# Moving the forget gate and the first head's maxima among the attention projections

## The chip, the core and the metric

The kernel runs on one core of one Trainium2 chip. Its engines work side by side: TensorE (PE: matrix products, PEld: the loading of weights), VectorE (DVE), ScalarE (ACT), GpSimd (POOL) and SyncE (SP, which mostly issues transfers). The metric is the device time of one execution in microseconds (us), as a median over runs.

## The reference, cut to what matters

One layer of a hybrid encoder, with 1024 frames of width 1024. From one normalised input `h` come three groups, whose outputs go through an output projection and a mixture of experts:

```
h = rms_norm(x); proj = h @ w_in
ya = rglru_group(...)               # gated linear recurrence, width 256
yb = fox_group(q, k, v, fl, ...)    # attention with a forget gate, 8 heads of 64
yc = rwkv7_group(...)               # delta rule with a matrix state, 4 heads of 64
x  = x + concat(ya, yb, yc) @ w_out
x  = x + hier_moe(rms_norm(x))

# inside fox_group
qh, kh = rms_norm(q), rms_norm(k)                 # per head
log_f  = log_sigmoid(f_logit + fb)                # 8 logits per frame
c      = cumsum(log_f, axis=1)                    # over the frames
s      = qh @ kh.T * scale + c[query] - c[key]
p      = softmax(where(key <= query, s, -inf));  o = p @ v
```

The change touches only when the 8 logits, their running sums `c` and the row maxima of the first head's scores are computed.

## The kernel before, in words

The RWKV group is worked in two passes, `rwkv(0)` and `rwkv(1)` (line 400), of two heads each. A pass begins with elementwise work on DVE and ACT (from the decay's sigmoid L420 and its running sum, the scan L422, to the products L445 to L455), then takes 8 groups of products L467, whose results DVE masks (L470), turns blocks (L477), and inverts 32 small triangular matrices at once by 31 dependent pairs of DVE operations (L485, L487: "the inverse"). The inverse goes out to DRAM and comes back in another layout (L490, L509, L514), DVE turns it (L519), and PE combines its parts (L523, L528, L537). Then comes the recurrence over 16 chunks: L578, L580, L586, L587, L588, L591, L595, L597, L599, each waiting for the one before on another engine, and at the end the output (L567, L616, L617).

A pass leaves PE much idle time. So PE's stream is written out by hand: `dense()` (line 872) is a generator of other work for PE, the filler, and `dfill(t)` (line 902) takes from it, between two steps of the pass, as much as the step's yield names. A step of the recurrence yields 0.75 (`WC`), and takes 8 matmuls. What a piece overshoots is not carried over to the next step. PE runs in program order; the order on the other engines is made by a scheduler from priorities, in which the steps of the pass stand ahead of the filler.

The last part of the filler is six attention projections in the order q0, k0, v0, q1, k1, v1 (`attn_proj`, line 728; 0 and 1 are heads 0 to 3 and 4 to 7). Each has 8 tiles `t` of 128 frames, 24 matmuls L741 a tile, 192 in all. After each quarter come the norm or the copy of its results (L760 to L776, L751 to L754), through 4 PSUM banks (`PB`) that the projections share with the pieces below. `mids` are pieces that run just ahead of a tile `t`; `FMT` says at which tiles of each projection, and `seq` in which order they come:

- `lru_norm1`, `lru_norm2` (L703): the recurrence group's norm. `lru_norm2` transposes 2 x 4 tiles (L708) into two banks in turn, and DVE multiplies with them (L710).
- `forget1` (L781): the logits, 128 small matmuls L790, then on ACT and DVE the softplus (L795 to L797, and L258 to L278 inside `softplus`: 27 operations on DVE), which ends in the tile `spf`. It yields 4.0.
- `forget2` (L804): the running sums, L807 and L808 on `spf`; on DVE 7 dependent additions L812 and L814 to L818.
- `forget3` (L822): their transposes (L826), copied by L828 and stored to DRAM (`crd`, L829).
- `fload0` (L844): loads the first head's queries and keys, transposed (L847 to L851), from what the projections q0 and k0 and `forget3` stored.
- nine pieces `fmax0` (L854): scores of the first head (L861), reduced by DVE to row maxima (L864).
- `wo_first`: loads weights of the output projection.

After the last filler come the attention heads: `fox_pre` loads the first head's operands in SP's queue (L947 to L957, among them `q3` and `kh`, which lie in space that the RWKV passes had), `fox_shift` closes the maxima (L983), `fox_max` starts on the next head (L968), `fox_av` forms scores (L996, L997) and `fox_pv` multiplies with the values (L1025).

Of the kernel before, what the change touches and what calls it, by code (L numbers as in the profile page):

```python
# [39 lines left out]
W3 = 1.6  # L40
W2 = 1.0
FMC = (((7, 0),), ((7, 1),), ((6, 0),), ((6, 1), (0, 0)), ((5, 0),), ((5, 1), (1, 0)), ((4, 0),), ((4, 1), (2, 0)), ((3, 0),))
FMT = ((2,), (4,), (0, 5), (0, 2, 7), (1, 3, 5, 7), (0, 1, 3, 5, 6))
NPS = ()
FSM = False
WC = 0.75
# [66 lines left out]
def hybrid_layer(ctx: ExitStack, tc: tile.TileContext, d, out):  # L113
# [255 lines left out]
    def low_rank():  # L369
        ps = yield from inproj_T(0)  # L370
        lr = Q()
        shifted(ps, 0, lr)
        A.activation(lr[0:32], lr[0:32], AF.Tanh)
        A.activation(lr[64:128], lr[64:128], AF.Sigmoid)
        for j, (a, b, c) in enumerate(((0, 32, 64), (32, 64, 64), (64, 128, 0))):
            A.activation(ls[a:b, j], lr[a:b], AF.Copy, scale=LS)
            V.scalar_tensor_tensor(ls[c:c + b - a, j], lr[a:b], LS, ls[a:b, j], op0=ALU.mult, op1=ALU.subtract)
        V.tensor_copy(ls[32:64, 0], ls[0:32, 0])
        V.tensor_copy(ls[0:32, 1], ls[32:64, 1])

    def in_k(ct, res, mids={}):
        kt_ = T(pr, [P, S], F32, "kraw")
        ps = yield from inproj_T(1 + 3 * ct, mids)
        shifted(ps, 1 + 3 * ct, kt_)
        res[ct] = [kt_, None, None]

    def in_r(ct, res, mids={}):
        rt_ = T(pr, [P, S], F32, "rraw")
        ps = yield from inproj_T(2 + 3 * ct, mids)
        shifted(ps, 2 + 3 * ct, rt_)  # L390
        res[ct][1] = rt_

    def in_v(ct, res, mids={}):
        vt_ = T(pr, [P, CH + S], F32, "vt")
        G.memset(vt_[:, 0:CH], 0.0)
        ps = yield from inproj_T(3 + 3 * ct, mids)
        shifted(ps, 3 + 3 * ct, vt_[:, CH:])
        res[ct][2] = vt_
# [243 lines left out]
    def gate_a(ct):  # L642
        ps = PB2()
        mm2(ps, wab[:, ct], xcs[ct], 0, P)
        for hf in range(2):
            A.activation(rs_[ct][:, HS[hf]], ps[hf], AF.Sigmoid, bias=vec("ba", ct))
        yield 1.7
# [24 lines left out]
    def lru_out(ct):  # L672
        ps = yield from inproj_T(9 + ct)
        r = rs_[ct]
        for hf in range(2):
            A.activation(r[:, HS[hf]], ps[hf], AF.Gelu_apprx_tanh, scale=1.0 / WS)
        V.tensor_tensor(hss[ct], hss[ct], r, op=ALU.mult)
# [194 lines left out]
    def dense():  # L872
        yield from low_rank()
        yield from in_k(0, ins)
        yield from in_r(0, ins)
        yield from in_v(0, ins)
        yield from lru_x(0)
        yield from lru_x(1)
        ga = [{MK[0]: lambda c=c: gate_a(c), MK[1]: lambda c=c: gate_b(c)} for c in range(2)]
        yield from in_k(1, nxt, ga[0])  # L880
        yield from in_r(1, nxt, ga[1])
        yield from lru_out(0)
        yield from lru_out(1)
        yield from in_v(1, nxt)
        ins[1] = nxt[1]
        yield from lru_norm()
        fm = [lambda c=c: fmax0(*c) for c in FMC]
        seq = [lru_norm1, lru_norm2, forget1, forget2, forget3, fload0] + fm + [wo_first]
        i = 0
        for j, (a, b) in enumerate(((0, 0), (1, 0), (2, 0), (0, 1), (1, 1), (2, 1))):  # L890
            m = {}
            for t in FMT[j]:
                m[t] = seq[i]
                i += 1
            yield from attn_proj(a, b, m)
        fst["post"] = seq[i:]
        wload_o(3)
# [941 lines left out]
```

## Time and profile before

| | |
|---|---|
| median of 3 runs | 911.71 us (910.83 to 913.49) |
| the profiled execution | 909.1 us, of which its span 907.3 us |
| busy in the span: PE, DVE | 823.9 us (91%), 631.0 us (70%) |
| busy in the span: ACT, POOL | 502.3 us (55%), 291.9 us (32%) |
| mean granted clock of PE | 0.945 of full speed |
| the pass `rwkv(1)` in the span, with the six projections as filler | from about 230 to 416 us |

A profile gives each engine's busy time; "idle before <- releaser" beside a row is the time for which an engine stood still before it, and what ended that. PEclk is the clock that was granted to PE: 1.00 is 2.4 GHz, 0.50 is 1.2 GHz. The page's chain of what ended last has here only the last transfer, so it says nothing of the stretch in question; the tables by window and the timelines do.

### The profile page before, as it was taken

Reading aid. Unit: us, or ns where it says so; the run is one execution under the profiler, and the core shown is the slowest. Engines: PE = TensorE matmul, PEld = TensorE weight load, DVE = VectorE, ACT = ScalarE, POOL = GpSimd, SP = SyncE. Lnnn points to the kernel's source line nnn. Section 1 sums busy time; section 2 is a strip of 40 time slices with the busy share of each in tenths; the row PEclk is TensorE's granted clock in tenths of the full one; section 3 lists DMA queues with packets and bytes.
Section 4 is the critical chain, followed back from the end, with each engine's and each line's share of the span. In section 5 each row is a group of like instructions: output and inputs, shape, how many; then the busy total and the mean of one; then the engine's idle time right before and its main releaser. Section 6 shows DMA issues by size and latency. Waiting matters only on the chain. (4 is left out here: it accounts for less than half of the span.)

```text
span 907.3 us, 19706 instructions
## 1 busy us (share of the span) xinstructions
PE 823.9 (91%) x8028; PEld 566.2 (62%) x8028; DVE 631.0 (70%) x1366; ACT 502.3 (55%) x776; POOL 291.9 (32%) x222
## 2 busy tenths in 40 slices
PE   7999989999979699999799999889699999999992
PEld 5644445447757577767466556545478788788771
DVE  6858973534699914555578987588949888868640
ACT  6772456554743133433677778676536766767730
POOL 1000001165372431430334443400034455566351
PEclk9999997999999789999899999989779999999996
DMA  9201030111021260215967755888736999999862
GB/s 332 66 25 47 24 72 11 47 48 48 24 84 38 78 119 25 71 48 123 239 150 162 165 130 122 310 314 327 297 108 239 340 351 357 339 357 346 262 97 46
DMA packets 98130, 144.95 MB, mean 160 GB/s; under 512 B 52544, under 2 KB 73920, under 8 KB 91888
## 3 DMA queue, kind: packets, MB, share of 16 engines
q1 hardware_dynamic: 89520, 117.71, 40.8%
q0 software_dynamic: 8080, 25.17, 11.5%
q8 instruction: 65, 1.06, 0.5%
q10 hardware_dynamic: 432, 0.74, 0.2%
q14 instruction: 33, 0.27, 0.1%
HBM read 97.54 MB, written 35.18 MB: 146 GB/s over the span
## 5 line engine op out<-in xcount | busy, mean ns | idle before, releaser
L741 PE MATMUL pb<-w,h 128*128 128x256 f16 x1152 | 147.7, 281 | 0.0
L1535 PE MATMUL pg<-tg,e 128*128 128x192 f16 x1536 | 137.5, 248 | 0.0
L1535 PEld LDWEIGHTS <-e 128*128 128x128 f16 x1536 | 126.9, 99 | 6.2 <-issue 5.8
L333 PE MATMUL pb<-h,w 128*128 128x512 f16 x528 | 129.7, 390 | 0.0
L741 PEld LDWEIGHTS <-h 128*128 128x128 f16 x1152 | 110.6, 101 | 22.2 <-issue 2.2
L1187 DVE SCALAR_TENSOR_TENSOR e<-est,go,e 128x2048 f16<-128x2048 f32 x36 | 83.5, 2346 | 2.5 <-ACT e L1186 2.5
L333 PEld LDWEIGHTS <-w 128*128 128x128 f16 x528 | 49.0, 100 | 56.4 <-issue 8.1
L1186 ACT ACTIVATE e<-est,go 128x2048 f16<-128x2048 f32 x36 | 70.8, 1995 | 17.7 <-PE pg L1535 17.2
L1011 POOL TENSOR_TENSOR ptl<-pfx,pth 128x512 f16<-128x512 f32 (+1 forms) x48 | 49.6, 1033 | 78.7 <-ACT pth L1010 45.8
L1001 ACT ACTIVATE pfx<-s,bia 128x512 f32<-128x512 f32 (+1 forms) x96 | 55.9, 582 | 32.1 <-PE s L997 19.3
L1472 POOL DMA_INDIRECT g<-td,gi x16 | 24.9, 1558 | 113.3 <-DVE oh L1315 73.3
L1590 POOL DMA_INDIRECT out_dram<-ya,si x16 | 39.5, 2471 | 61.7 <-ACT ya L1589 58.9
L1065 PE MATMUL op<-w,y 128*128 128x512 f16 x192 | 59.3, 391 | 0.0
L971 DVE TENSOR_REDUCE mx<-m 128x1 f32<-128x512 f32 (+2 forms) x84 | 44.7, 552 | 16.1 <-PE m L970 12.4
L245 POOL TENSOR_SCALAR wst<-wst 128x1024 f32<-128x1024 f32 x12 | 34.7, 2896 | 57.1 <-DMA wst<-in_wq_dram 56.8
L1484 ACT COPY tg<-tr 128x1024 f16<-128x1024 f16 (+2 forms) x34 | 26.5, 800 | 43.7 <-PE tr L1490 43.6
L1595 POOL DMA_INDIRECT out_dram<-yb,si x16 | 45.5, 2842 | 11.9 <-DVE yb L1594 9.2
L1010 ACT ACTIVATE pth<-s,bia 128x512 f16<-128x512 f32 (+1 forms) x80 | 47.1, 589 | 0.0
L1238 PE MATMUL pa<-wo,yf 128*128 128x512 f16 x192 | 46.5, 391 | 0.0
L247 POOL TENSOR_TENSOR w<-wst,w 128x1024 f16<-128x1024 f32 x12 | 27.3, 2287 | 59.4 <-ACT w L246 59.2
L1576 PE MATMUL pa<-e,hd 128*128 128x512 f16 x192 | 44.1, 379 | 0.0
L1025 PE MATMUL ob<-v,pth 128*128 128x65 f16 x288 | 37.1, 196 | 1.2 <-DMA v<-vd 1.2
(402 smaller groups left out, 1774.5 us busy)
## 6 DMA issues: line engine op xcount, KB each, us to landing
est<-in_wgu_dram SPq DMA_DIRECT2D x32, 1024.0 KB
est<-in_wdn_dram SPq DMA_DIRECT2D x16, 1024.0 KB
wst<-in_wq_dram SPq DMA_DIRECT2D x12, 512.0 KB
wst<-in_wt_dram SPq DMA_DIRECT2D x11, 512.0 KB
xt<-in_x_dram SPq DMA_DIRECT2D x8, 512.0 KB
xp<-in_x_dram SPq DMA_DIRECT2D x8, 512.0 KB
xpd<-xp SPq DMA_DIRECT2D x8, 512.0 KB
y<-xpd SPq DMA_DIRECT2D x8, 512.0 KB
```

Source lines behind the costliest of these rows:

```text
L333: PE.matmul(ps[hf], w[:, wi, k, :], hT[hf][:, hi, k, :], start=(k == 0 and wi == 0 and hi == 0), stop=(k == NK - 1 and wi == 1))
L741: PE.matmul(ps[:, ti * 256:(ti + 1) * 256], hT[t // 4][:, hi, k, (t % 4) * P:(t % 4) * P + P], w[:, wi, k], start=(k == 0 and hi == 0 and ...
L971: V.tensor_reduce(mxs[h][:, i, qt:qt + 1], sp, axis=AX.X, op=ALU.max)
L1001: A.activation(pfx, sp, AF.Exp, bias=bia[:, kt, h:h + 1])
L1010: A.activation(pth, sp, AF.Exp, bias=bia[:, kt, h:h + 1])
L1011: (G if seg in KPL else V).tensor_tensor(ptl, pfx, pth, op=ALU.subtract)
L1065: PE.matmul(ps, yT[k][:, yi, qs], wo[k // 2][:, wi, k % 2, cs], start=(k == 0 and yi == 0 and wi == 0), stop=(k == 7 and yi == 1))
L1186: A.activation(w[:, 0], st, AF.Copy, scale=sc)
L1187: V.scalar_tensor_tensor(w[:, 1], st, sc, w[:, 0], op0=ALU.mult, op1=ALU.subtract)
L1238: PE.matmul(ps[:, HF[hf]], yT[k][:, yi, qs], wo[k // 2][:, wi, k % 2, HF[hf]], start=(k == order[0] and yi == 0 and wi == 0), stop=(k == o ...
L1535: PE.matmul(pg[gu][:, cs], wk[:, wi, k % 4, c0:c0 + P], tg[0][:, tg[1], hi, k], start=(k == 0 and wi == 0 and hi == 0), stop=(k == NK - 1 ...
L1595: dma = G.indirect_dma_start(out2, IOA(ap=si[:, 2 * j + 1:2 * j + 2], axis=0), yb, None, compute_op=ALU.add, bounds_check=2 * ROWS - 1)
```

## The change

Two tables change. In `seq` the piece `forget1` comes first, `forget2` between the two halves of the recurrence group's norm. In `FMT` the positions are new: `forget1` moves from the head of v0 to the head of q0, `forget2` from v0 tile 5 to k0 tile 1, `forget3` from q1 tile 0 to k0 tile 6, `fload0` from q1 tile 2 to v0 tile 3. The nine maxima stood at q1 tile 7, k1 tiles 1, 3, 5, 7 and v1 tiles 0, 1, 3, 5; now they stand at q1 tiles 0, 3, 6, k1 tiles 0, 3, 6 and v1 tiles 0, 2, 4. `lru_norm1` (q0 tile 2), `lru_norm2` (k0 tile 4) and `wo_first` (v1 tile 6) stay.

```diff
-FMT = ((2,), (4,), (0, 5), (0, 2, 7), (1, 3, 5, 7), (0, 1, 3, 5, 6))
+FMT = ((0, 2), (1, 4, 6), (3,), (0, 3, 6), (0, 3, 6), (0, 2, 4, 6))
...
-        seq = [lru_norm1, lru_norm2, forget1, forget2, forget3, fload0] + fm + [wo_first]
+        seq = [forget1, lru_norm1, forget2, lru_norm2, forget3, fload0] + fm + [wo_first]
```

On DVE, before, the softplus of the logits (L796, L797, L258, ...; `fu` are the logits, `sp_` its tiles) stands between the pairs of the inverse of `rwkv(1)`:

```order
L765 TENSOR_TENSOR a_345_2441<-pb_2449,qss_2650 128x512
L485 TENSOR_TENSOR q_357_2514<-q_356_2510,q_357_2514 128x5x22
L796 TENSOR_TENSOR fu_2805<-fu_2805,pb_2676 128x64
L487 TENSOR_TENSOR q_357_2514<-q_357_2514 128x5x22
L797 SCALAR_TENSOR_TENSOR fu_2805<-fu_2805,brow_125 128x64
L485 TENSOR_TENSOR q_357_2514<-q_356_2510,q_357_2514 128x6x21
L258 TENSOR_SCALAR sp_a_2810<-fu_2805 128x64
L487 TENSOR_TENSOR q_357_2514<-q_357_2514 128x6x21
L259 TENSOR_TENSOR sp_a_2810<-sp_a_2810,fu_2805 128x64
```

In the changed kernel the same operations stand on DVE among the last chunks of the recurrence of `rwkv(0)` (L580, L587 and L599 are its steps):

```order
L580 SCALAR_TENSOR_TENSOR npv_2000<-rb_1801,q_188_1272 128x64
L796 TENSOR_TENSOR fu_1960<-fu_1960,pb_1831 128x64
L797 SCALAR_TENSOR_TENSOR fu_1960<-fu_1960,brow_125 128x64
L258 TENSOR_SCALAR sp_a_1965<-fu_1960 128x64
L259 TENSOR_TENSOR sp_a_1965<-sp_a_1965,fu_1960 128x64
L587 COPY q_151_919<-rb_2012 64x64
L265 TENSOR_SCALAR sp_d_1970<-sp_e_1968 128x64
L266 RECIPROCAL sp_d_1970<-sp_d_1970 128x64
L599 SCALAR_TENSOR_TENSOR zbd_86_415<-rb_2017,gl_628,zg_2002 128x64
L268 TENSOR_TENSOR sp_z_1973<-sp_e_1968,sp_d_1970 128x64
```

The softplus has left the inverse, and its 27 operations stand in the recurrence that runs before it.

On DVE, before, the running sums (L812 to L818) stand behind the inverse's last pair, and the copy of their transposes (L828) ahead of the turn L519:

```order
L485 TENSOR_TENSOR q_357_2514<-q_356_2510,q_357_2514 128x16
L487 TENSOR_TENSOR q_357_2514<-q_357_2514 128x16
L812 TENSOR_TENSOR ex_2975<-ex_2975,pb_2972 128x8 x7
L814 TENSOR_TENSOR ncq_2984<-pb_2972,ex_2975 128x64
L815 TENSOR_SCALAR bia_427<-ncq_2984 128x64
L817 TENSOR_SCALAR cst_2987<-ncq_2984 128x64
L818 SCALAR_TENSOR_TENSOR cst_2987<-ncq_2984,cst_2987 128x64
L752 SCALAR_TENSOR_TENSOR a_393_3014<-pb_2947,a_393_3014 128x8x64
L828 COPY crow_3091<-pb_3082 16x1024
L519 STREAM_TRANSPOSE q_369_2644<-q_367_2635 32x512 x2
```

Now they stand in the elementwise part of `rwkv(1)`, between its products (L449, L455) and the projections' and norm's operations (L765, L710, L763):

```order
L447 TENSOR_TENSOR kraw_1040<-kraw_1040,q_330_2333 128x1024
L812 TENSOR_TENSOR ex_2432<-ex_2432,pb_2429 128x8
L449 TENSOR_TENSOR q_338_2400<-kraw_1040,q_328_2318 128x8x64
L449 TENSOR_TENSOR q_339_2401<-kraw_1040,q_328_2318 128x8x64
L455 SCALAR_TENSOR_TENSOR rraw_1123<-rraw_1123,pv_100,kraw_1040 128x1024
L254 RECIPROCAL qss_2371<-qss_2371 128x8
L812 TENSOR_TENSOR ex_2432<-ex_2432,pb_2429 128x8
L765 TENSOR_TENSOR a_322_2287<-pb_2295,qss_2371 128x512
L812 TENSOR_TENSOR ex_2432<-ex_2432,pb_2429 128x8 x4
L710 TENSOR_TENSOR a_177_1106<-a_177_1106,pb_2539 128x512
L812 TENSOR_TENSOR ex_2432<-ex_2432,pb_2429 128x8
```

So seven additions, four further operations and, later among the L470, the copy L828 come ahead of the inverse.

In SP's queue, before, the inverse's transfers (L490, L509, L514) come ahead of the store of the running sums (L829) and of the first head's transposed loads (L847, L848):

```order
L776 DMA kd_421<-a_346_2442 128x4x512
L754 DMA vd_422<-a_386_2891 128x4x516
L490 DMA t_358_2578<-q_357_2514 1024x1x32 x2
L509 DMA q_367_2635<-t_358_2578 32x32x32 x2
L514 DMA q_368_2638<-t_358_2578 32x16x32 x4
L754 DMA vd_422<-a_393_3014 128x4x516
L829 DMA crd_423<-crow_3091 16x1024
L177 DMA wst_4051<-in_wq_dram 128x8x128
L847 DMA_TRANSPOSE a_413_3261<-qd_420 128x1024
L848 DMA_TRANSPOSE a_413_3261<-kd_421 128x1024
```

Now they come behind them:

```order
L829 DMA crd_423<-crow_2664 16x1024
L177 DMA wst_3566<-in_wq_dram 128x8x128
L177 DMA wst_4026<-in_wq_dram 128x8x128
L847 DMA_TRANSPOSE a_394_2950<-qd_420 128x1024
L776 DMA kd_421<-a_364_2647 128x4x512
L849 DMA a_394_2950<-in_qr_dram 4x1024
L848 DMA_TRANSPOSE a_394_2950<-kd_421 128x1024
L850 DMA a_394_2950<-crd_423 2x1024
L851 DMA a_394_2950<-in_qr_dram 2x1024
L754 DMA vd_422<-a_392_2921 128x4x516
L490 DMA t_375_2769<-q_374_2705 1024x1x32 x2
```

On SP the loads L847 and L848, and what each waits for, have moved ahead of the inverse's transfers.

On PE the filler up to the last output of `rwkv(1)` (L616) is longer by 32 matmuls L741: before, 105 of them were left behind it, now 73, while one piece `fmax0` that was behind it is now ahead. Ahead of the first step of `rwkv(1)` (L409) there are 142 matmuls L741 instead of 150. At L523 of `rwkv(1)`, 631 are done instead of 600, and one `fmax0`. From L523 to L616 there are 447 before and 448 now, with 8 pieces `fmax0` each.

## Rows read from the trace of the kernel before

**Rows 1.** Windows: length, busy of PE, PEld, DVE, ACT, POOL; clock; DMA share, GB/s

```profile
206.00:239.00 33.00, 31.60 (x297) 25.39 (x296) 15.54 (x36) 18.81 (x35) 12.69 (x9) 1.00 0.16 49
240.00:278.00 38.00, 31.56 (x263) 24.69 (x261) 36.11 (x46) 16.36 (x21) 23.54 (x10) 0.96 0.18 56
278.00:325.00 47.00, 38.74 (x399) 32.16 (x400) 39.95 (x114) 12.72 (x19) 16.89 (x10) 0.85 0.26 63
```

**Rows 2.** Timeline of PE: start, us, line, operands, count, idle before

```profile
258.60 1.09 PE L708 MATMUL pb<-cf,a 128*128 128x128 f32 x4 [5.42 <-DVE a L765]
...
284.84 3.35 PE L790 MATMUL pb<-wf,h 128*128 128x16 f16 x128
...
310.55 0.66 PE L807 MATMUL pb<-spf,cf 128*128 128x64 f32 x2 [7.57 <-DVE spf L278]
...
324.96 2.21 PE L523 MATMUL ra<-q,ma 32*32 32x32 f32 x64
```

**Rows 3.** Timeline of DVE in rwkv(1), from the scan to the turn

```profile
239.36 2.29 DVE L422 TENSOR_TENSOR_SCAN q<-smask,q 128x1024 f32<-128x1024 f16 x1 [2.95 <-ACT q L420]
...
278.08 3.89 DVE L477 STREAM_TRANSPOSE q<-ma 32x1024 f32<-32x1024 f32 x2
...
291.24 1.86 DVE L485 TENSOR_TENSOR q<-q,q 128x110 f32<-128x110 f32 x1
...
302.80 0.36 DVE L485 TENSOR_TENSOR q<-q,q 128x128 f32<-128x128 f32 x1
...
303.55 0.37 DVE L485 TENSOR_TENSOR q<-q,q 128x135 f32<-128x135 f32 x1
...
314.04 1.33 DVE L812 TENSOR_TENSOR ex<-ex,pb 128x8 f32<-128x8 f32 x7
...
322.34 0.68 DVE L828 COPY crow<-pb 16x1024 f16<-16x1024 f16 x1 [4.46 <-PE pb L826]
322.95 1.28 DVE L519 STREAM_TRANSPOSE q<-q 32x512 f32<-32x512 f32 x2
```

**Rows 4.** Timeline of DVE in the inverse of rwkv(0), and behind it

```profile
110.18 0.37 DVE L485 TENSOR_TENSOR q<-q,q 128x126 f32<-128x126 f32 x1
...
110.91 0.40 DVE L485 TENSOR_TENSOR q<-q,q 128x136 f32<-128x136 f32 x1
...
125.83 0.19 DVE L487 TENSOR_TENSOR q<-q 128x16 f32<-128x16 f32 x1
...
132.78 1.29 DVE L519 STREAM_TRANSPOSE q<-q 32x512 f32<-32x512 f32 x2 [2.24 <-DMA q<-t]
```

**Rows 5.** Timeline of POOL

```profile
209.11 4.21 POOL L247 TENSOR_TENSOR w<-wst,w 128x1024 f16<-128x1024 f32 x2 [3.77 <-ACT w L246]
...
290.84 2.12 POOL L247 TENSOR_TENSOR w<-wst,w 128x1024 f16<-128x1024 f32 x1 [2.06 <-ACT w L246]
```

**Rows 6.** Windows behind L790, and behind L523 of rwkv(0); columns as in Rows 1

```profile
289.00:292.00 3.00, 3.00 (x16) 2.13 (x14) 2.93 (x8) 2.45 (x4) 1.16 (x1) 0.50 0.55 163
...
135.00:138.00 3.00, 3.00 (x29) 1.61 (x26) 0.18 (x1) 1.93 (x2) 0.36 (x1) 0.54 0.56 165
```

**Rows 7.** Timeline of PE, from the last output of rwkv(1) to the first head

```profile
415.14 0.38 PE L616 MATMUL rb<-ls,lrw 128*128 128x512 f16 x1
...
420.31 8.02 PE L741 MATMUL pb<-w,h 128*128 128x256 f16 x72
428.26 0.61 PE L983 MATMUL s<-id,mst 128*4 128x128 f16 x8
...
433.90 0.27 PE L968 MATMUL m<-k,q 68*128 68x128 f16 x1 [1.49 <-DMA k<-kh]
...
440.65 0.19 PE L1025 MATMUL ob<-v,pth 128*128 128x65 f16 x1 [1.22 <-DMA v<-vd]
```

**Rows 8.** Timeline of SP's queue at the first head's loads

```profile
418.96 0.37 SPq L754 DMA_DIRECT2D vd<-a  x1
...
421.20 1.24 SPq L948 DMA_TRANSPOSE kh<-kd  x1
```

## Prediction

> **What bounds the kernel now.** I read the page's busy shares first (PE is busy nearly throughout, so time can be won only where PE waits or runs at its lower clock), then PE by stage, then the timelines of PE, DVE and SP around the moved pieces. The reader is to see four things.
>
> While the recurrence of rwkv(0) ends, PE is busy for 31.60 of 33 us at full clock [rows 1]. Work put there costs its own time.
>
> From 278 to 325 us PE is busy for 38.74 of 47 us at a mean clock of 0.85 [rows 1]. Most of what is missing is one wait: L807 stands 7.57 us for the softplus [rows 2]. That is the stall which the change is about.
>
> DVE goes through the pass rwkv(1) from the scan L422 at 239.36 to the blocks' turn L477 at 278.08, busy for 36.11 of 38 us on the way [rows 1], and on to the end of the inverse, where L812 begins at 314.04 [rows 3]. The end of the inverse sets when its transfers start, and these set L519 and L523. In rwkv(0) it is 6.76 us from the last pair's end (125.83 + 0.19) to L519 [rows 4]. I take 0.75 us from there to L523, an estimate from half of L519 (two turns in 1.28 us) and a little for the hand-over. So in rwkv(1) L523 could begin at 314.04 + 6.76 + 0.75 = 321.55; PE comes to it at 324.96 [rows 2]: 3.4 us of slack. L519 was itself held up by L828, which stands ahead of it and waited 4.46 us for PE [rows 3].
>
> At the end, the last output L616 stands at 415.14, 13.1 us of filler and output follow, L983 starts at 428.26, and then PE waits for transfers (1.49 us at L968, 1.22 us at L1025) [rows 7]. Of these the chain in SP's queue is the cause: L754 at 418.96, and behind it the loads up to L948 at 421.20 [rows 8].
>
> So the 7.57 us are not there to be taken. What counts is when the DVE chain of rwkv(1) ends, since the recurrence, its last output and the first head hang on it; filler that PE does earlier is only filler that it lacks later.
>
> **The change part by part.**
>
> 1. *The logits at the head of q0.* The 128 matmuls L790 take 3.35 us [rows 2], now ahead of the start of rwkv(1), where PE has no idle time to hide them. Behind them before, PE was busy for all of 289 to 292 us at a clock of 0.50, its 1.2 GHz level [rows 6]: 3 us busy for 1.5 us of work, so 1.5 us lost. I take that loss along; it is between 0 and 1.5. The Trainium skill (TensorE: Matmul & The Clock Gate, Why this matters for your kernels) says to avoid drops by leaving no idle gaps between bursts of matmuls; by that, L790, which leaves none, would cost no clock, and this sum would be 1.5 smaller. The trace differs, since the lower clock comes right behind it without a gap. Eight matmuls L741 fewer stand ahead of L409, at 8.02 us for 72 [rows 7] or 0.11 each: -0.9. The softplus on DVE and ACT, and its table load, now lie among steps of the recurrence; I take 0.4, with 0 and 3.4 as ends (rival 3). Sum: 3.35 + 1.5 - 0.9 + 0.4 = +4.4 for L422, which starts at 239.36 [rows 3]. Own range 2.5 to 5.5.
>
> 2. *The running sums ahead of the inverse.* L812 takes 1.33 us for seven dependent additions [rows 3], 0.19 each; with L814 to L818 at the same price, eleven make 2.1. L828 takes 0.68 [rows 3]. Before, eleven stood behind the inverse, where DVE had time, and L828 ahead of L519. Now all twelve stand in the stretch from L422 to L477, with 1.9 us of gaps on DVE to take them [rows 1]. There are also hand-overs: the norm's first half now takes a bank that q0's last quarter must leave by L765, its second half the bank that L814 must leave, and L467 and the transposes L826 alternate. PE's wait of 5.42 us [rows 2] at the second half splits into several of about the same sum. I count 0.8 for DVE's waits on PE. Sum: +3.6, from 1.6 (all sums in gaps, L828 and hand-overs alone) to 4.5.
>
> 3. *The inverse without the softplus.* Twenty-seven operations leave it, at 0.19 each 5 us of busy time. But the pairs depend on each other, and the softplus ran in the bubbles between them: from one L485 to the next it took 303.55 - 302.80 = 0.75 us with softplus operations between [rows 3], and 110.91 - 110.18 = 0.73 us in rwkv(0) without them, at the same size [rows 4]. So 0.02 a pair, and -0.3 for the some 15 pairs concerned; the bounds are 0 and -5.
>
> 4. *The stall and L523.* L807's wait goes. PE arrives at L523 early and waits there instead. By 1 to 3 the inverse ends 4.4 + 3.6 - 0.3 = 7.7 us later; 3.4 of it is slack that PE had, and L828 no longer stands ahead of L519. L523 begins 4.3 us later, at about 329.3. By then PE has done 31 more matmuls L741 (3.4 us) and one piece of the maxima.
>
> 5. *The clock behind the new wait.* In rwkv(0), where PE had waited before L523, the clock was 0.54 from 135 to 138 us with PE fully busy [rows 6]. Before, rwkv(1) had only a part of this at L523. I take +1.5, between 0 and 2.7, for the pieces L523 to L537 that the recurrence waits for.
>
> 6. *The tail.* From L523 to L616 the filler is the same, 448 matmuls for 447. So L616 comes at 415.14 + 4.3 + 1.5 = 420.9, 5.8 later. Behind it 73 matmuls L741 are left for 105, and the one piece of the maxima has gone ahead: 1.3 for L616 and L617 (four rows of the 0.38 of L616, overlapping) and 73 x 0.11 = 8.1. L983 begins at 430.3, 2.0 later.
>
> 7. *The first head's loads.* Before, L947 could be issued only behind L754 at 418.96, and L948 at 421.20 [rows 8]. L948 writes space that the last L567 of the pass reads, less than 1 us ahead of L616, so it may now start at 420.9 at the earliest, about its old time. Its own waiting vanishes: the old release of the queue (a quarter of v1) comes earlier now. So the transfers land where they did, and L1025 at 440.65 moves by -0.2 to +0.3. L968 would follow L983 at the old distance of 5.64 less its wait of 1.49, 4.15 [rows 7]: at 434.5, +0.6; from there to L1025 PE has 440.65 - 1.22 - 433.90 = 5.5 us of work, so it is at L1025 at 440.0 and still waits for v. Sum of the change: +0.3.
>
> The mechanism is linear: about +5.6 us at L616 are free, because 32 matmuls and a piece of the maxima have left the tail and SP's queue is released earlier; each us less or more at L616 shows at the end.
>
> Against the profiled execution (909.1 us; its span and 1.8 us around it) this gives 909.4. The median of the runs shown is 2.6 above that execution, so the forecast is 911.7 + 0.3 = 912.0 us: no change. 0.3% is 2.7 us, about what a measurement can tell from none.
>
> **The rivals.**
>
> 1. *Cheap moves, faster: 908.5.* The clock does not fall behind L790 (-1.5), and the sums fit between other DVE operations (-2.0): L616 3.5 earlier than in my sum. For it: where L790 will stand, small matmuls of the recurrence run among L741 at a clock of 1.00 [rows 1]. Against it: the clock right behind L790 [rows 6], and DVE's lack of gaps [rows 1].
>
> 2. *The whole softplus counts, faster: 907.* The inverse shortens by the 5 us of busy time, -4.7 against my sum. Against it: the two periods of 0.75 and 0.73 us [rows 3, 4].
>
> 3. *The softplus slows the recurrence of rwkv(0), slower: 915.4.* POOL has two L247 there, 4.21 us from 209.11 on [rows 5], about when the softplus would run. In the inverse, L485 at 291.24 took 1.86 us and ended with the POOL operation that had begun at 290.84 [rows 5, 3], against some 0.37 for such an operation otherwise [rows 3]. The Trainium skill (GPSIMD Engine Reference, Key points) says that GpSimd shares its SBUF interfaces with VectorE, with contention for DVE instructions with two SBUF inputs; L485 is one, and the trace agrees. L259, L268 and the L274 are such operations too, and L599, the step that PE waits for, is queued behind them; L259 stands ahead of L587. One POOL operation is 2.1 us, and the table load that the softplus's exponential needs on ACT (1.3, an estimate: somewhat under half of the 2.95 us that L422 waited for the sigmoid behind such a load [rows 3]) stands ahead of L588. Price: 3.4 us at L422, all of it lost to the end. It decides from +7 us at L422 on, in place of +4.4.
>
> 4. *The loads in SP's queue hold up the inverse, slower: 916.* L847 and L848 now stand ahead of L490. If L848's wait for the stored keys lasts beyond the inverse's end, L490 goes late by it, some 4 us. For it: the order. Against it: k0's last matmul stands right ahead of L790 at 284.84 before [rows 2], 29 us ahead of the inverse's end.
>
> That the change doesn't do what it says would show as L807 waiting still; the softplus would have to last beyond k0 tile 1, which is 216 matmuls L741, some 24 us at 0.11 each, behind L790.
>
> **How the numbers follow.** Forecast 0.42, its own range 909.0 to 915.0; rival 1 0.24; rival 2 0.05; rival 3 0.24; rival 4 0.05. The range for 8 in 10 leaves out most of rival 2 and the outer parts of 1, 3 and 4: 908.0 to 916.4. Faster than 909.0: 0.24 x 0.7 + 0.05 + 0.42 x 0.07 = 0.25. Slower than 914.4: 0.24 x 0.85 + 0.05 x 0.9 + 0.42 x 0.12 = 0.30. Within: 0.45.
>
> **What would show it.** Step 1: L790 at about 207 us, a clock of 0.50 behind it, and L422 at 243.8; at 242 rival 1, at 246.5 or later rival 3, with a DVE operation of the softplus of 1 us or more beside POOL's L247. Step 2: 42.3 us from L422 to L477 instead of 278.08 - 239.36 = 38.7, and waits of PE at both halves of L708. Step 3: still some 32 us from the end of L477 to that of the inverse (278.08 + 3.89 to 314.04 [rows 3]). Step 4: no wait at L807, and one of several us at L523 for L519. Steps 6 and 7: L616 at 421, L983 at 430.3, L1025 at about 441. I am wrong if L616 moves by other than 3 to 8.5 us, or if the time at L1025 does not carry to the end.

## The result, and the profile after

The changed kernel takes 917.0 us (median of 17 runs, 914.39 to 922.15), against 911.2 us for the kernel before in the same rounds; the ratio is 1.0061 (1.0045 to 1.0077). It is slower by some 5.6 us. The forecast was 912.0 with a range up to 916.4, so the time lies above the range, and "no change" was missed too.

The profiled execution has a span of 913.6 us, 6.3 more than before. PE has the same 8028 instructions and is busy for 0.4 us more:

```profile
PE 824.3 (90%) x8028; PEld 566.6 (62%) x8028; DVE 641.3 (70%) x1366; ACT 501.6 (55%) x776; POOL 290.7 (32%) x222
```

DVE is busy for 10.3 us more than in the table of the kernel before, with the same 1366 instructions. That is the first hint: DVE operations took longer, none was added.

By windows of the same sense as [rows 1] (the head of q0 to the scan L422, from there to L477, and on to L523; columns as there):

```profile
206.00:245.50 39.50, 36.81 (x415) 29.25 (x413) 25.15 (x63) 21.73 (x39) 12.78 (x9) 0.91 0.14 41
245.50:288.00 42.50, 34.45 (x274) 26.30 (x273) 37.78 (x59) 16.73 (x22) 22.47 (x10) 0.88 0.16 51
288.00:334.00 46.00, 36.87 (x301) 30.79 (x301) 39.65 (x74) 11.66 (x17) 19.47 (x11) 0.93 0.30 71
```

The first stretch, which ran at a clock of 1.00 before, now has a mean of 0.91. The timeline of PE, answering to [rows 2]:

```profile
206.06 3.35 PE L790 MATMUL pb<-wf,h 128*128 128x16 f16 x128
...
209.61 1.72 PE L741 MATMUL pb<-w,h 128*128 128x256 f16 x8
...
218.54 0.51 PE L595 MATMUL rb<-q,ma 128*64 128x64 f32 x3 [0.79 <-DVE q L587]
...
265.03 1.09 PE L708 MATMUL pb<-cf,a 128*128 128x128 f32 x4 [4.82 <-DVE ex L812]
267.78 1.09 PE L708 MATMUL pb<-cf,a 128*128 128x128 f32 x4 [1.67 <-DVE ncq L814]
...
318.07 0.38 PE L861 MATMUL pb<-a 68*128 68x512 f16 x1 [1.02 <-DVE q L487]
325.47 8.01 PE L741 MATMUL pb<-w,h 128*128 128x256 f16 x55 [7.03 <-DVE a L752]
334.14 2.29 PE L523 MATMUL ra<-q,ma 32*32 32x32 f32 x64 [0.66 <-DVE q L519]
```

L790 stands where the change put it, and the eight L741 behind it take 1.72 us instead of the 1.05 that eight take at the upper clock. The wait of 7.57 us at L807 is gone. In its place PE waits 7.03 us ahead of the L741 at 325.47, for a copy (L752) that stands on DVE among the pairs of the inverse; at L523 itself it waits 0.66 us. The chain on DVE, answering to [rows 3]:

```profile
210.98 2.02 DVE L258 TENSOR_SCALAR sp_a<-fu 128x64 f32<-128x64 f32 x1
...
217.52 0.95 DVE L275 TENSOR_SCALAR sp_acc<-sp_acc 128x64 f32<-128x64 f32 x1
217.63 0.84 DVE L587 COPY q<-rb 64x64 f32<-64x64 f32 x1
...
245.55 2.29 DVE L422 TENSOR_TENSOR_SCAN q<-smask,q 128x1024 f32<-128x1024 f16 x1 [2.36 <-ACT q L420]
...
287.95 3.90 DVE L477 STREAM_TRANSPOSE q<-ma 32x1024 f32<-32x1024 f32 x2
...
293.02 0.20 DVE L485 TENSOR_TENSOR q<-q,q 128x31 f32<-128x31 f32 x1
...
318.11 0.35 DVE L485 TENSOR_TENSOR q<-q,q 128x108 f32<-128x108 f32 x1
...
318.79 2.15 DVE L485 TENSOR_TENSOR q<-q,q 128x96 f32<-128x96 f32 x1
320.97 2.06 DVE L487 TENSOR_TENSOR q<-q 128x96 f32<-128x96 f32 x1
...
327.02 0.19 DVE L487 TENSOR_TENSOR q<-q 128x16 f32<-128x16 f32 x1
...
333.39 1.29 DVE L519 STREAM_TRANSPOSE q<-q 32x512 f32<-32x512 f32 x2 [4.39 <-DMA q<-t]
```

The inverse runs from 293.02 to 327.21, 34.2 us, though the softplus has left it; before it ran from 283.14 to 314.13, 31.0 us:

```profile
283.14 0.20 DVE L485 TENSOR_TENSOR q<-q,q 128x31 f32<-128x31 f32 x1
...
313.94 0.19 DVE L487 TENSOR_TENSOR q<-q 128x16 f32<-128x16 f32 x1
```

Two of its operations near the end take 2.15 and 2.06 us, where the pair just ahead of them took 0.35 and 0.27. POOL's timeline, answering to [rows 5], shows what stands beside them:

```profile
208.74 4.21 POOL L247 TENSOR_TENSOR w<-wst,w 128x1024 f16<-128x1024 f32 x2 [3.78 <-ACT w L246]
215.65 5.51 POOL L245 TENSOR_SCALAR wst<-wst 128x1024 f32<-128x1024 f32 x2 [2.70 <-DMA wst<-in_wq_dram]
...
318.70 4.22 POOL L247 TENSOR_TENSOR w<-wst,w 128x1024 f16<-128x1024 f32 x2 [2.21 <-ACT w L246]
```

The last row is the pair of subtractions that makes the low half of k1's weights. It may begin when PE has done with v0, which used that buffer: here at 317.05, the end of the last L741 of v0.

```profile
305.75 11.30 PE L741 MATMUL pb<-w,h 128*128 128x256 f16 x102
```

In the kernel before, v0 ended at 321.76, and this pair ran from 323.41 to 327.62, behind the inverse:

```profile
323.41 4.21 POOL L247 TENSOR_TENSOR w<-wst,w 128x1024 f16<-128x1024 f32 x2 [19.22 <-ACT w L246]
```

The end, answering to [rows 7] and [rows 8]:

```profile
426.36 0.38 PE L616 MATMUL rb<-ls,lrw 128*128 128x512 f16 x1
...
435.70 0.61 PE L983 MATMUL s<-id,mst 128*4 128x128 f16 x8
...
446.50 0.19 PE L1025 MATMUL ob<-v,pth 128*128 128x65 f16 x1 [0.91 <-DMA v<-vd]
```

```profile
424.62 0.37 SPq L754 DMA_DIRECT2D vd<-a  x1
...
427.22 1.24 SPq L948 DMA_TRANSPOSE kh<-kd  x1
```

Executions begin q0 at slightly different times (204.2 to 209.8 us over all profiles here), so I count from the start of q0, that is from its first matmul, L790 or L741. In the kernel before that is 206.44. The stages of all runs, in us from there, with the ratio of the times:

| kernel | L422 | inverse, length | L523 | L616 | L1025 | ratio to before (95%) |
|---|---|---|---|---|---|---|
| before | 32.9 | 31.0 | 118.5 | 208.7 | 234.2 | 1 |
| changed | 39.5 | 34.2 | 128.1 | 220.3 | 240.4 | 1.0061 (1.0045 to 1.0077) |
| e8 changed, again | 39.4 | 34.2 | 128.1 | 220.4 | 240.7 | 1.0066 (1.0041 to 1.0090) |
| e1 k1 off POOL | 39.2 | 30.6 | 124.5 | 216.8 | 237.1 | 1.0047 (1.0029 to 1.0066) |
| e2 logits alone | 39.4 | 32.3 | 125.6 | 214.2 | 235.8 | 1.0056 (1.0025 to 1.0086) |
| e3 maxima back | 39.2 | 34.2 | 128.4 | 222.8 | 242.4 | 1.0111 (1.0077 to 1.0145) |
| e4 logits in the stall | 32.9 | 30.3 | 120.3 | 211.0 | 237.3 | 1.0083 (1.0055 to 1.0111) |
| e5 softplus alone | 37.0 | 34.2 | 125.9 | 218.1 | 239.6 | 1.0078 (1.0056 to 1.0101) |
| e6 logits spread | 34.2 | 35.0 | 123.4 | 216.9 | 243.9 | 1.0097 (1.0059 to 1.0136) |
| e7 spread, alone | 34.6 | 30.8 | 115.3 | 208.3 | 236.8 | 1.0021 (1.0000 to 1.0043) |
| e9 maxima alone | 32.9 | 31.0 | 119.1 | 209.8 | 237.3 | 1.0042 (1.0019 to 1.0066) |
| e10 sums later | 32.9 | 34.8 | 118.6 | 214.3 | 239.4 | 1.0088 (1.0057 to 1.0119) |
| e11 later, spread | 32.9 | 34.6 | 118.6 | 214.5 | 240.7 | 1.0068 (1.0039 to 1.0096) |
| e12 later, k1 off POOL | 34.1 | 31.0 | 116.0 | 210.7 | 236.7 | 1.0033 (1.0008 to 1.0058) |
| e13 later, k1 on DVE | 34.2 | 30.3 | 115.4 | 211.2 | 236.0 | 1.0057 (1.0032 to 1.0082) |
| e14 and PE kept busy | 35.7 | 30.2 | 117.5 | 207.2 | 232.5 | 0.9981 (0.9962 to 1.0000) |
| e15 busy in both | 32.9 | 30.3 | 115.1 | 210.2 | 235.4 | 1.0026 (1.0005 to 1.0046) |

Two profiles of the changed kernel agree within 0.3 us in each stage; the stages behind L1025 differ more from one execution to the next (from L1025 to the first matmul of the output projection L1238 it is 139.8 to 145.8 us over all profiles, and from there to its last 57.7 to 60.4). So causes are read from the stages, and the ratio says only what reaches the end. One relation holds over all 17 profiles: where k1's pair on POOL begins inside the inverse, the inverse is 34.2 to 35.0 us long (32.3 in e2, where it meets only the end), and everywhere else 30.2 to 31.0.

### The profile page after: what moved, and what is told of

Same layout as the page of the kernel before. It is cut to its first block, busy times and chain, and to the rows that moved or that the text cites. A ratio compares the mean times of both kernels' runs of the same rounds, so it can differ in the third digit from the quotient of the medians.

```text
span 913.6 us, 19701 instructions
## 1 busy us (share of the span) xinstructions
PE 824.3 (90%) x8028; PEld 566.6 (62%) x8028; DVE 641.3 (70%) x1366; ACT 501.6 (55%) x776; POOL 290.7 (32%) x222
## 5 line engine op out<-in xcount | busy, mean ns | idle before, releaser
L741 PE MATMUL pb<-w,h 128*128 128x256 f16 x1152 | 149.6, 285 | 8.0 <-DVE a L752 7.0
L741 PEld LDWEIGHTS <-h 128*128 128x128 f16 x1152 | 111.9, 102 | 31.3 <-issue 9.8
L1472 POOL DMA_INDIRECT g<-td,gi x16 | 29.7, 1854 | 114.0 <-DVE oh L1315 73.7
L245 POOL TENSOR_SCALAR wst<-wst 128x1024 f32<-128x1024 f32 x12 | 34.5, 2888 | 70.9 <-DMA wst<-in_wq_dram 70.8
L1590 POOL DMA_INDIRECT out_dram<-ya,si x16 | 36.5, 2284 | 60.4 <-ACT ya L1589 57.3
L1238 PE MATMUL pa<-wo,yf 128*128 128x512 f16 x192 | 46.0, 388 | 0.0
L247 POOL TENSOR_TENSOR w<-wst,w 128x1024 f16<-128x1024 f32 x12 | 27.1, 2277 | 42.0 <-ACT w L246 37.6
L1025 PE MATMUL ob<-v,pth 128*128 128x65 f16 x288 | 36.6, 194 | 0.9 <-DMA v<-vd 0.9
```

The source lines that it names most:

```text
L741: PE.matmul(ps[:, ti * 256:(ti + 1) * 256], hT[t // 4][:, hi, k, (t % 4) * P:(t % 4) * P + P], w[:, wi, k], start=(k == 0 and hi == 0 and ...
L1238: PE.matmul(ps[:, HF[hf]], yT[k][:, yi, qs], wo[k // 2][:, wi, k % 2, HF[hf]], start=(k == order[0] and yi == 0 and wi == 0), stop=(k == o ...
```

## The experiments

**e1, k1's subtractions off POOL.** On the changed kernel:

```diff
-split(st, hi, lo, WS, PSPL and (which, hh, i) not in NPS)
+G.tensor_scalar(st, st, WS, ...); A.copy(hi, st); A.activation(lo, st, AF.Copy, scale=0.0)   # for k1
```

> The changed kernel, with one thing taken away: the low half of k1's weights is no longer a subtraction on POOL (L247) but a store of zeros by ACT, so those low halves are left out of the product. Theory A (the inverse of rwkv(1) grew from 32.2 to 35.4 us because k1's pair of subtractions, 4.22 us from 318.70, now falls into its end, where before it came behind it): the inverse is 31 to 31.5 us long, L523 comes 4 us earlier than 334.14, at about 330, and the time is 912.5 to 913.5. Theory R (the inverse grew because all POOL work beside it is aligned otherwise, and taking one pair away only lets the next transfer or operation fill its place): the inverse stays above 34 us and the time within 1 us of 917.

Measured: the inverse runs from 295.36 to 325.97, 30.6 us, 3.6 less; L523, L616 and L1025 come 3.3 to 3.6 us earlier. In the profile of e1, POOL has no subtraction between 312 and the end of the inverse, and the operations at its end are short:

```profile
295.36 0.20 DVE L485 TENSOR_TENSOR q<-q,q 128x31 f32<-128x31 f32 x1
...
325.78 0.19 DVE L487 TENSOR_TENSOR q<-q 128x16 f32<-128x16 f32 x1
```

The ratio fell from 1.0061 or 1.0066 to 1.0047; the intervals overlap, so the time alone would not show it, and the expected time (912.5 to 913.5, beside 911.2 for the kernel before a ratio of some 1.002) was missed. The stages do show it: theory A holds, and nothing else filled the place. Two things more can be read here. Without the pair the inverse is 0.4 us shorter than in the kernel before: so much, at most, the leaving softplus was worth. And PE's wait for L752 is 3.54 us instead of 7.03, so about half of it was POOL's doing:

```profile
324.23 8.24 PE L741 MATMUL pb<-w,h 128*128 128x256 f16 x55 [3.54 <-DVE a L752]
```

**e2, the logits alone.** On the kernel before:

```diff
-FMT = ((2,), (4,), (0, 5), (0, 2, 7), ...)
+FMT = ((0, 2), (4,), (5,), (0, 2, 7), ...)   # forget1 first in seq
```

> The kernel before, with forget1 alone moved to the head of q0; forget2, forget3, the loads and the maxima stay. Theory A (three costs: 6.2 us at the head of rwkv(1) from forget1, 3.7 us between L422 and L477 from the running sums, 3.2 us in the inverse from k1's subtractions on POOL): L422 at 245.5, 38.7 us from L422 to L477 as before, L807 without a wait, an inverse lengthened by 0 to 2 us since v0's end comes later against it; L616 2 to 6 us later than in the kernel before and L1025 3 us earlier to level; 908.5 to 912.5. Rival (the head of q0 costs all, since everything else only follows it): L616 and the time as in the changed kernel, 916 to 917.5.

Measured: L422 as late as in the changed kernel, 38.0 us from L422 to L477 (42.4 in the changed kernel), L807 without a wait, the inverse 32.3 us. L616 is 5.5 us later than before and L1025 1.6. Both costs that the theory separates are seen: the head of q0 costs 6.5 us at L422, the sums cost another 4 between L422 and L477, and only in the changed kernel. The time, 1.0056, is above what I expected, by more than the first head shows; why is left open.

**e3, the maxima put back.** On the changed kernel, `FMT = ((0, 2), (1, 4, 6), (3,), (7,), (1, 3, 5, 7), (0, 1, 3, 5, 6))`.

> The changed kernel, with the nine maxima back at their old tiles (q1 7, k1 1 3 5 7, v1 0 1 3 5); the head of the change (forget1, forget2, forget3, fload0) stays. Theory A says the spread of the maxima is worth nothing: one more piece lies behind L523 (0.4 us) and 72 matmuls L741 and one piece lie behind L616 as against 73 and none: 916.5 to 918. Rival (the spread costs, since in the changed kernel PE waits at L861, at L586 and for 7 us behind the first of the maxima): 914 to 916.

Measured: all the same up to L519, then 94.4 us from L523 to L616 against 92.2, since PE now waits 7.47 us directly at L523 and the lower clock follows there. L1025 is 2.0 us later. The theory had given the spread nothing; it is worth 2 us here: with a maximum at q1 tile 0 PE waits earlier, and the clock is up again by L523. The time (1.0111) is above both expectations.

**e4, the logits in PE's stall.** On the kernel before, forget1 at k0 tile 3 (`FMT = ((2,), (3, 4), (5,), (0, 2, 7), ...)`).

> The kernel before, with forget1 alone moved to tile 3 of k0, ahead of the norm's transposes, where PE had waited 5.42 us; all else stays. L422 stays at 239.4, L790 costs no time of its own, the wait of 7.57 us at L807 goes or shrinks below 2 us, and about half of the softplus lies between L422 and L477, which grows by 0.5 to 2.5 us. Theory A: v0 ends on PE at some 311 to 313 us, so k1's subtractions on POOL fall into the inverse, which grows by 1.5 to 3.5 us and eats what was won: 909.5 to 913. Rival R (POOL's pair there does not matter): L523 3 us earlier than 324.96 and 907 to 909.

Measured: L422 unmoved and L790 free, as expected. But L422 to L477 took 43.2 us instead of 38.7: the scheduler put 16 of the 27 operations of the softplus there. The inverse was no longer than before (30.3), so that part of the expectation missed: k1's pair begins at 320.48, behind the inverse's end at 317.85. The time (1.0083) is above the expectation, and by more than the 3.1 us at L1025. Of the three places tried for the softplus, the elementwise part of rwkv(1) is the dearest on DVE, and the inverse, where it had stood, the cheapest (at most 0.4 us, e1).

**e8, the changed kernel again, and e5, the softplus without POOL beside it.** In e5, k0's subtractions and v0's scaling are taken from POOL (`A.activation` in their place).

> The changed kernel once more, to stand beside the next three on one chip. All theories: a ratio to the kernel before of 1.004 to 1.009; the interval from the first L790 to L409 again some 32 us, the inverse again over 34.5 us.

> The changed kernel, with POOL's weight work taken from beside the softplus: k0's subtractions (POOL L247 at 208.74) are replaced by zeros from ACT, so that k0's low halves are left out of its product, and v0's scaling (POOL L245 at 215.65) is done on ACT. Theory A (of the 6 us at the head of rwkv(1), about 2 come from the softplus: DVE operations of it stood up to 2.0 us beside POOL, L587 came 0.8 us late, and PE's clock fell a second time behind that wait): from the first L790 to L409 29.5 to 30.8 us instead of 32.2, no DVE operation of the softplus above 0.6 us, no clock of 0.50 from 222 to 226; the time 1 to 3 us below the changed kernel's. Rival (it is L790 and its own clock drop alone): 31.5 to 32.5 us and a time within 1 us of the changed kernel's.

Measured in e8: 32.1 us from L790 to L409 and the ratio as expected, the inverse 34.2 us, a little under the expected 34.5. Measured in e5: from L790 to L409 29.7 us instead of 32.2; the wait at L587 is gone, and no operation of the softplus takes above 0.65 us. But of the two falls of the clock it was the first that was missing, and the second stayed, behind the 16 one-column matmuls L697 at 222.70 (window, busy and count, clock, DMA share, GB/s):

```profile
214.00:216.00 2.00, 2.00 (x29) 1.00 0.03 8
...
226.00:228.00 2.00, 2.00 (x16) 0.50 0.01 4
```

In the changed kernel both are there, the first right behind L790 without a gap:

```profile
210.00:212.00 2.00, 2.00 (x17) 0.50 0.00 0
...
224.00:226.00 2.00, 2.00 (x14) 0.50 0.00 0
```

So the 2.5 us are some 0.8 of wait and 1.7 of clock. In e5 the clock had been at 0.50 from 204.5 to 207.9 already, ahead of q0 (209.81), which no other profile shows; so that it held behind L790 is not shown to be POOL's doing, and is left open. The time did not follow (1.0078): 2.2 us of gain at L616 are 0.9 at L1025, where PE waited 2.2 us for v, and the time is later than the changed kernel's, which the expectation had excluded; the stages behind L1025 vary by as much.

**e6 and e7, the logits handed out one by one.** A `yield 0.026` behind each L790, and 0.01 for the 4.0 at the end: e6 on the changed kernel, e7 on e2.

> The changed kernel, with forget1's matmuls handed out one by one: each L790 yields 0.026, so that the steps of the recurrence take some 28 of them instead of 8 matmuls L741, in place of all 128 at one point. L409 then stands behind 100 matmuls L741 instead of 142. Theory A (the 3.35 us of L790 in one block delay the recurrence, and the block pulls the clock down): the clock stays at 1.00 behind them, from the first L790 to L409 26 to 29 us instead of 32.2; the burst from L422 to L477 stays at 42 us; L616 3 to 6 us earlier than in the changed kernel but 40 more matmuls L741 behind it; 911 to 914.5, or 2.5 to 6 us below the changed kernel. Rival (the softplus in the recurrence is what costs): 30 us or more and a time within 1.5 us of the changed kernel's.

> The kernel before with forget1 alone moved to the head of q0 and its matmuls handed out one by one; the running sums stay at v0 tile 5, the maxima where they were. Theory A: no cost at L422 beyond 1.5 us, 38.5 us from L422 to L477, no wait at L807, k1's subtractions on POOL behind or at the end of the inverse, L523 1 to 4 us earlier than 324.96; 0 to 4 us faster than the kernel before. Rival (softplus beside POOL's work in the recurrence costs more than the wait at L807 was worth): 1 to 4 us slower than the kernel before.

Measured: L422 is only 1.3 and 1.7 us later than before (34.2 and 34.6), with 100 matmuls L741 ahead of L409 instead of 142. But the clock did not stay up, as expected for e6: in e7 it is at its lower level from 207.6 to 221.3, while L790 are mixed in (206.4 to 212.9) and for 8 us behind them, although PE is hardly idle there, and in e6 from 210.8 to 221.0. One window of e7:

```profile
212.00:215.00 3.00, 3.00 (x47) 0.50 0.67 186
```

So it does not take the block for the clock to fall. e7 has the inverse at 30.8 us and L523 3.3 us earlier than before, as theory A said; from there to L616 it takes 93.0 us instead of 90.2, and behind L616 28.5 instead of 25.5, since fewer L741 had been done. It ends at 1.0021 (1.0000 to 1.0043), not faster as expected. In e6 PE waits 10.2 us at the first maximum, for the loads of `fload0`, which come too late for it, and the expected gain in time was missed (1.0097).

**e9, the maxima alone, on the kernel before** (`(0, 2, 4, 6), (0, 3, 6), (0, 2, 4, 5, 6)` for q1, k1, v1), **e10, the running sums later,** and **e11, both.** e10:

```diff
-FMT = ((2,), (4,), (0, 5), (0, 2, 7), ...)
+FMT = ((2,), (4,), (0,), (0, 2, 4, 7), ...)
```

> The kernel before with the maxima alone spread: q1 tiles 4 and 6, k1 tiles 0, 3, 6 and v1 tiles 0, 2, 4, 5, behind the loads, which stay at q1 tile 2; the forget gate stays. By the run with the maxima put back (which came 2 us later at L1025 than the changed kernel) the spread is worth something only through the maximum that stands at q1 tile 0, ahead of L523, and here none can stand there: within 1 us of the kernel before. Rival (an even spread as such saves 2 us in the recurrence): 1.5 to 2.5 us faster than the kernel before.

> The kernel before with the other answer to the wait at L807: the logits stay at the head of v0 and the softplus in the inverse, and forget2 goes later, to q1 tile 0, with forget3 and the loads at q1 tiles 2 and 4; the maxima stay. Theory A (nothing that DVE needs for the inverse is made longer, and v0 ends on PE at 311 to 314 us, so k1's subtractions on POOL stay behind the inverse's last pairs or touch the last of them): no wait at L807, the inverse 31 to 33 us, L523 1.5 to 3.5 us earlier than 324.96, a clock of 0.50 behind it for some 2 to 4 us, the first head 0 to 2.5 us earlier; 0 to 2.5 us faster than the kernel before. Rival B (PE's waits only change places: the wait comes back at L523, and what the recurrence wins it gives to the lower clock): L616 and the time within 1 us of the kernel before, or later.

> The one before with the maxima spread: q1 tile 6, k1 tiles 0, 3, 6 and v1 tiles 0, 2, 3, 4, 5. Theory A: as the run before, within 1 us of it, since no maximum can stand ahead of L523 here. Rival: another 1 to 2 us faster.

e9 missed: it is slower. A piece with two maxima in one bank lies behind L616, and PE waits 2.7 us between them for DVE's L864.

e10 is the run that explains most. L422, L477 and the softplus in the inverse are as before, and the wait at L807 is gone. Yet the inverse takes 34.8 us, because PE, not held at L807, ends v0 earlier, and k1's pair on POOL comes at 310.60:

```profile
310.60 4.21 POOL L247 TENSOR_TENSOR w<-wst,w 128x1024 f16<-128x1024 f32 x2 [8.30 <-ACT w L246]
```

Two operations of the inverse then take 2.11 and 2.03 us. So the wait at L807 had kept this pair behind the inverse. And PE waits 9.56 us at L523 instead, with the lower clock behind it, where the recurrence hangs on PE:

```profile
323.15 3.62 PE L523 MATMUL ra<-q,ma 32*32 32x32 f32 x64 [9.56 <-DVE q L519]
```

L523 takes 3.62 us instead of 2.21, and L523 to L616 95.7 us instead of 90.2. Rival B holds. e11 does much the same, with the wait in two parts (4.55 us for L752, 4.01 at L523).

**e12, e13 and e14: e10 with k1's pair off POOL,** without its low half (e12, the edit of e1) or made by ACT and DVE (e13, `NPS = ((1, 1, 0), (1, 1, 1))`), and e13 with PE kept busy (e14):

```diff
         yield WT[ct]
-        ps = RA()
+        ps = RA(); [PE.matmul(ps[:, 0:512], wz[:, 0:P], wz, start=True, stop=True) for _ in range(30 * ct)]
```

> The kernel with the running sums later (e10), and k1's subtractions taken off POOL: its low halves are zeros from ACT and so left out of the product. Theory A (the wait at L807 had kept k1's subtractions behind the inverse): the inverse 31 us instead of 34.8, L523 3.7 us earlier than in e10 against the start of q0 (114.9 us behind it, 118.6 in e10 and 118.5 in the kernel before); L523 to L616 94 to 96 us as in e10 since PE waits there still; about level with the kernel before, ratio 0.998 to 1.004. Rival (something else beside the inverse grew): the inverse above 33.5 us.

> As e12, but nothing left out: k1's halves come from ACT and DVE (L249, L250), which on DVE stand behind the inverse. Theory A: the inverse 31 us, L523 114.5 to 115.5 us behind the start of q0, L523 to L616 94 to 96 us; ratio to the kernel before 0.998 to 1.004. Rival: DVE's two L250 come into the inverse or ahead of L519 and cost 1 to 2.5 us there.

> As e13, with 30 extra matmuls of zeros (128 x 512, into the bank that L523 then overwrites) ahead of L523 of rwkv(1), to keep PE busy while it would wait. Theory C (behind a wait at L523 the clock is at its lower level for the pieces L523 to L537, on which the recurrence hangs): no clock of 0.50 in the 15 us behind L523, L523 to L616 88 to 91 us instead of 94 to 96, and a time 3 to 6 us below e13, that is 1 to 5 us below the kernel before. Rival (the recurrence is longer for another reason, its filler or its own waits): L523 to L616 above 93 us and a time within 1.5 us of e13.

Measured: the inverse is 31.0 and 30.3 us long, and L523 comes 2.6 to 3.2 us earlier than in e10: the pair on POOL was all that had lengthened the inverse. (e13's two L250 stand behind the inverse.) With PE still waiting at L523, L523 to L616 takes 94.7 and 95.8 us, and both are slower than the kernel before, e13 (1.0057) beyond its expected range. With the extra matmuls there is no wait at L523, the clock is up for the next 9.7 us, and the stretch takes 89.8 us:

```profile
317.36 6.64 PE L521 MATMUL ra<-wz 128*128 128x512 f16 x30
323.93 2.21 PE L523 MATMUL ra<-q,ma 32*32 32x32 f32 x64
```

```profile
324.00:327.00 3.00, 3.00 (x73) 1.00 0.85 224
...
334.00:336.00 2.00, 2.00 (x14) 0.50 0.00 0
```

Theory C holds but for one point: no fall at all was expected in these 15 us, and the clock is at 0.50 from 333.6 to 337.0. e14 wins 6.0 us from L523 to L616 against e13, less 2.1 at L523. Of these 1.5 lie ahead of L422: there e12, e13 and e14 have the stream of the kernel before on PE, and yet a fall of the clock behind L697 (3.4, 3.4 and 6.8 us long) which the kernel before did not have, with L422 later by 1.2 to 2.8 us. L1025 comes 3.5 us earlier than in e13; the medians differ by 7.4, more than the stages show. The other profiles bear theory C out: L523 to L616 takes 88.6 and 89.8 us where 1.7 us of work were lost to the lower clock in the 15 us behind L523 (e2, e14), 90.2 to 90.7 where 3.0 to 3.4 were (before, e4, e9; e6 stands apart with 93.5), 92.2 to 93.0 with 4.6 or 4.7, and 94.4 to 95.9 with 5.8 to 6.8. e14 has the lowest ratio of this study: 907.49 us, 0.9981 (0.9962 to 1.0000) against the kernel before, clearly below the changed kernel. Its interval reaches 1, so that it is faster than the kernel before is not shown.

**e15, PE kept busy in both passes,** with 11 extra matmuls in rwkv(0) and 26 in rwkv(1).

> As e14, with 26 extra matmuls instead of 30 ahead of L523 of rwkv(1), and 11 ahead of L523 of rwkv(0), where PE had waited 2.49 us. Theory C: no clock near 0.5 from 135 to 138 us, the stretch from L523 to L616 of rwkv(0) 1 to 3 us shorter, L523 of rwkv(1) some 0.7 us earlier than in e14; a ratio to the kernel before of 0.993 to 0.998. Rival (in rwkv(0) the clock falls on filler that nothing waits for, or falls again at once): ratio 0.996 to 1.000, no different from e14.

It missed, and shows the point once more. 26 were too few: PE waits 1.20 us at L523, the clock falls again, and L523 to L616 takes 95.1 us.

```profile
319.28 2.69 PE L523 MATMUL ra<-q,ma 32*32 32x32 f32 x64 [1.20 <-DVE q L519]
```

```profile
324.00:327.00 3.00, 3.00 (x40) 0.50 0.88 289
```

With four matmuls fewer, 0.9 us of work, this stretch is 5.3 us longer. In rwkv(0) the wait at L523 vanished, but PE waited 1.42 us at L528 for ACT instead and the clock fell there: from L523 to the first L578 15.7 us as against 15.8 before. Nothing was won.

## Why the prediction was wrong

Step by step, from the start of q0 (the forecast's steps against the profile after):

| step | forecast | measured |
|---|---|---|
| 1, L422 later by | +4.4 | +6.6 |
| 2, L422 to L477 longer by | +3.6 | +3.7 |
| 3, the inverse longer by | -0.3 | +3.2 |
| 3 and 4, L523 later by | +4.3 | +9.6 |
| 5, L523 to L616 longer by | +1.5 | +2.0 |
| 6 and 7, given back behind L616 | 5.5 | 5.4 |
| L1025 later by | +0.3 | +6.2 |

Much of the mechanism was right: the wait at L807 is not there to be taken, the DVE chain of rwkv(1) sets when L523 begins, the sums cost what step 2 said, and some 5.5 us at L616 are free. Two terms were wrong.

Step 3 is the one that failed. It asked what the softplus takes out of the inverse, and there it was about right (0.3 forecast, 0.4 by e1 against the kernel before). It put at nothing, without a reason, what the removed wait lets in. I had cited that L485 stands still to the end of a POOL operation [rows 3, 5], and used it only for rival 3, in another place. The changed kernel ends v0 on PE at 317.05 while the inverse runs to 327.21; before, v0 ended at 321.76, 7.6 us behind the inverse's end. Whoever sets the start of the buffer's next user against the new end of the inverse sees the pair fall in. e1 shows that it costs 3.6 us, e10 that taking the wait away is enough to bring it in, and e12 and e13 that removing the pair is enough to undo it.

Step 1 was mis-sized. It had L790 (3.35, as measured), one fall of the clock (1.5; 1.7 measured) and 0.4 for the softplus. There were two falls of the clock. The accounts of PE's windows give 3.4 us of work lost to the lower clock from the start of q0 to L422 in both profiles of the changed kernel, and none before; the second fall lies behind L697, which had stood at the same tile before without one. Whether the change brings that second fall is open: the changed kernel has it in both profiles, but e12, e13 and e14 have one behind L697 too, with the logits at their old place. The wait at L587 (0.8 us), less waits that went, is about the 0.4.

Two smaller points did not come as said. Step 4 had PE wait several us at L523; it waited 0.66 us there, and 7.03 ahead of it, for L752 (3.54 without k1's pair, e1). And rival 4 did not come: from the inverse's end to L519 it is 6.2 us, not more than the 6.76 of the sum. (Two figures of the forecast do not add up, and nothing hangs on them: the lower end of step 2 is 1.5, not 1.6, and what is free at L616 is 5.8 less 0.3, 5.5 and not 5.6.)

Rival 3 named a slower result near the measured time, but it is not what happened. DVE did stand still beside POOL in the softplus, for up to 2.02 us (L258), and PE lost 0.8 us by it, not 3.4; L422 stayed under the +7 us from which it was to decide. The Trainium skill (GPSIMD Engine Reference, Key points) names two kinds of DVE instructions that contend with GpSimd, those in a 2-port performance mode and those with two SBUF inputs. I used only the second. L258 and L275 have one input and stood still beside POOL too; whether they run in that mode no row shows.

Rival 1 relied on no fall of the clock behind L790, and rival 2 on a shorter inverse; neither came. The rule of the Trainium skill on the clock (TensorE: Matmul & The Clock Gate, Why this matters for your kernels), to leave no idle gaps between bursts, does not describe L790: behind it the clock fell without a gap, and in e7 it was at its lower level for 13.7 us with PE nearly always busy. It does describe L523 in e13 (a wait of 5.82 us, and the lower clock) against e14 (neither there), but the Trainium skill means longer gaps than the 1.20 us of e15, behind which the clock fell as well.

There is one more lesson in the accounts. From the start of q0 to L1025, PE was idle for 26.2 us before and 28.8 after, and lost 12.0 us to the lower clock before and 16.7 after (sums over windows of 1 us of the time not busy, and of busy time by one less the granted clock). The change took out a wait of 7.57 us and PE's idle time grew. A wait of about the same length came back ahead of 325.47, half of it because DVE was held up by POOL.

## What to carry to other kernels

Before a wait is taken away, look at what it holds back: the engine that waits frees buffers later, and what these release on other engines (here two subtractions on POOL) may fall on the chain that sets the end. A wait beside other engines' critical work, with its low clock spent on filler, may be the cheapest place for it; a wait in front of the pieces that everything hangs on lowered the clock for them, and filling it with matmuls of zeros won 6.0 us in the stretch behind it (e14 against e13). Of a wait's length nothing is won until the chain that ends behind it gets shorter.

## What was not expected of the hardware

A wait of 1.20 us at L523, with the small matmuls L523, L528 and L537 behind it, was followed by a clock of 0.50 from 320.7 to 337.8 (e15); with no wait at the same place, behind 30 matmuls of zeros, the clock was at 1.00 for the next 9.7 us and then at 0.50 for 3.4 (e14). The 128 matmuls L790 of 16 and 8 columns went with the lower clock while they ran among others (e6, e7), and in one block in most profiles too, with the fall right behind the block or already in it; in e4, e5, e11 and e14 none came within 4 us of its end. L790 themselves hardly take longer at the lower clock: 3.52 us in e1, where it was at 0.50 for most of them, against 3.35. DVE operations with one input stood still beside POOL too: L258 took 2.02 us beside the subtraction L247, and of the six L275 beside the scaling L245 three took 0.69 to 1.03 us and three the usual 0.2.
